# Conditioning chunks tied behind one weight split each, and the seven products of the values in another order

## The chip, the cores and the metric

The kernel runs on one core of a Trainium2 chip, in one launch. The metric is the device time in microseconds (us) of that launch; smaller is better. The engines meant below are TensorE (matmuls), the vector engine (VectorE), the scalar engine (ScalarE), GpSimd, and SyncE, which here does nothing but issue transfers. Each engine takes its instructions from a queue of its own, in order.

## The reference

Two layers of a block on 512 tokens of 1024 numbers each, float32 throughout. Layer 0 mixes tokens with a gated linear recurrence, layer 1 with dilated attention in three groups; each is followed by a gated feed-forward. Every norm is scaled, shifted and gated by a conditioning vector, which is a matrix of 1024 by 6144 times one vector:

```python
for layer in range(DEPTH):
    mod = (cond @ ada_w[layer] + ada_b[layer])[:, None, :]
    sh1, sc1, g1, sh2, sc2, g2 = jnp.split(mod, 6, axis=-1)
    u = rms_norm(h, norm_g[layer, 0]) * (1.0 + sc1) + sh1
    ...
    h = h + (1.0 + g1) * rms_norm(y, norm_g[layer, 1])
    u = rms_norm(h, norm_g[layer, 2]) * (1.0 + sc2) + sh2
    y = swiglu_ffn(u, ffn_w_in[layer], ffn_w_out[layer])
    h = h + (1.0 + g2) * rms_norm(y, norm_g[layer, 3])
```

The change lies in layer 1's attention:

```python
proj = (u @ w_in).astype(jnp.float32).reshape(B, S, N_GROUPS, 3, ATT_HEADS, ATT_HEAD_DIM)
for gi, (window, dilation) in enumerate(DILATED_GROUPS):
    q = apply_partial_rope(proj[:, :, gi, 0], cos, sin) * scale
    k = apply_partial_rope(proj[:, :, gi, 1], cos, sin)
    v = proj[:, :, gi, 2]
    o_g, lse_g = dilated_group_attention(q, k, v, window, dilation)
    ...
wts = jax.nn.softmax(jnp.stack(lses, axis=0), axis=0)
o = jnp.einsum('gbsh,gbshd->bshd', wts, jnp.stack(outs, axis=0))
```

with eight heads of 128 and the groups (128, 1), (512, 4) and (2048, 16).

## The kernel before

**Numbers.** A float32 product is made of three TensorE products of parts. A scalar-engine copy rounds a weight to a high part (`hi`, L123), a vector-engine subtraction gives the low part (`lo`, L124), and `three` (L446) issues hi by hi, hi by lo and lo by hi. So the last parts that a block of matmuls waits for are the low parts of its weights.

**Weights.** `Stream` holds one list of items for the whole program, in the order in which they are wanted. A "w" item is a weight tile of 1 MB: loaded by SyncE's queue into one of two raw tiles, then split into one of three pairs of parts. A "unit" is a block of the values' weights of 1024 by 512, in two tiles. An "ada" item is a chunk of a conditioning matrix (256 rows by 512 columns in this stage), a "rows" item a bias and norm row for a gate, a "do" item work without a load. `process_to` (L112) works through the list: where it meets a weight, it splits it; where it meets another item, it calls the item's function. `weave` puts the conditioning items among the weights: after weight number `first + n * every`, group n. For the weights of q and k the pair (first, every) is `ADA_AT` (L35).

**Conditioning beside q and k.** 24 chunks, two vector-engine products each (L282 for the first of a sum, else L284, 128x512), make six half vectors: scale, shift and gate of the second half of layer 1. When a half vector's eight products are done, GpSimd adds it over the partitions (L286), and a later item writes it into columns (L301) or, for the gate, into a row (L336, L337). During this stage the chunks have two tiles of their own ("side" tiles, from the pool opened as `a_side`), so they don't take raw tiles from the weights; `fill` loads into them as soon as one of the two is free, and `place` remembers which items were loaded so.

**Values, 680 to 781 us.** The product of 512 tokens by 1024 with 1024 by 512 weights is done per unit in the manner of Strassen, with seven products p1 to p7 of quarter size (24 matmuls of 256 columns each) instead of eight. Each needs a weight quarter or a sum of quarters: p1 takes q1, p2 and p3 take q3 (p3 after S4), p4 q2, p5 the sum S1 (L1605, here on the vector engine only for the second unit, on GpSimd for the later ones), p6 S2 (L1611, which needs S3, L1608), and p7 the q0 that S3 overwrote; S4 is L1614. `parts` splits such a quarter (scalar copy, then the low part `loq` on the vector engine, L1628). The products land in banks that are put together by `keep2`, `keep3` (scalar copies), `add4` (L1661) and `add5` (L1665) on the vector engine, `add1` (L1669) on GpSimd, and `out11`, `out12`, `out21`, `out22` (L1672 to L1681) on the vector engine. This stage is written out by hand: the four compute engines run it in the order of the calls.

**Heads, 781 to about 1150 us.** For each of 24 (head, group) pairs, one weight tile gives q and k (two blocks of 24 matmuls of 512 columns, L447 to L449), the scalar engine moves them out of the banks (L1827, L1828), the vector engine turns the first 32 rows (L1835 to L1838, "turning"), and two scalar copies (L1841) put these back into q and k. `Fillers` calls, a fixed number of blocks later, the scores (L1870 for the plain group, L1889 for the two others), their maxima (L1875, L1891) and exponentials, the merging of the groups (weights from L1910 on, products at L1926 and L1933), the transposes (L1938) and the products with V (L1963 to L1975). The order of calls is only a start here: the framework's scheduler works out with a model of its own in which order each engine gets these instructions, so the recorded order may differ from that of the code.

Of the kernel before, what the change touches and what calls it, by code (L numbers as in the profile page):

```python
# [9 lines left out]
F32 = mybir.dt.float32  # L10
# [23 lines left out]
R0 = 0  # L34
ADA_AT = (1, 0.85)  # L35


class Stream:
# [75 lines left out]
    def process_to(self, end):  # L114
        while self.done < end:
            self.fill()
            i = self.done
            kind = self.items[i][0]
            t = self.raw.pop(i)
            if kind == "w":  # L120
                hi = self.pool.tile([P, 2048], F32R, name=f"hi{i}", tag="hi", bufs=self.parts)
                lo = self.pool.tile([P, 2048], F32R, name=f"lo{i}", tag="lo", bufs=self.parts)
                self.nc.scalar.copy(hi, t)  # L123
                self.nc.vector.tensor_sub(lo, t, hi.bitcast(F32))  # L124
                self.ready.append((hi, lo))
            else:
                self.items[i][2](t)
# [63 lines left out]
def block_kernel(tc, x, c, positions, ada_w, ada_b, norm_g, hgrn_w_in, lower, hgrn_norm_g, hgrn_w_out,  # L191
# [6 lines left out]
    with ExitStack() as ctx:  # L198
# [223 lines left out]
        st = Stream(nc, wp, items, 2, 3)  # L422
        st.side_end = side_end

# [1127 lines left out]
        def values(turn):  # L1552
# [166 lines left out]
            b = Unit(UNITS[1])  # L1719
            b.S1(dve)  # L1720
            a.keep3()
            a.run("p6")
            b.S3()
            b.parts("p1")
            a.add4()
            a.add1()
            a.run("p7")
            b.S2()
            b.parts("p5")
            b.parts("p6")  # L1730
            a.add5()
            a.out12()
            a.run("p4")
            for n in range(1, len(UNITS)):
                last = a
                a, b = b, None
                a.hold()
                a.run("p1")
                a.parts("p2")
                last.out21()  # L1740
                a.run("p6")
                a.S4()
                a.keep2()
                last.out22()
                a.parts("p7")
                a.run("p5")
                a.parts("p3")
                a.add4()
                a.run("p2")
                a.keep3()  # L1750
                a.add1()
                a.parts("p4")
# [6 lines left out]
                a.run("p7")  # L1759
                a.out11()  # L1760
                if b:
                    b.parts("p1")
                    b.S3()
                a.run("p3")
                a.add5()
                if b:
                    b.S2()
                    b.parts("p6")
                a.run("p4")
                a.out12()  # L1770
                if b:
                    b.parts("p5")
            a.out21()
# [263 lines left out]
```

## Time and profile before

| what | value |
|---|---|
| time, median of 3 runs | 1526.21 us (1524.43 to 1528.13) |
| profiled execution, its own time | 1522.11 us |
| its span | 1520.4 us |
| mean granted TensorE clock | 0.997 |
| values stage | 680 to 781 us |
| heads stage | 781 to about 1150 us |

A row of the page's fifth part gives a group of instructions by line, engine and tile, its count, busy time and mean, and the idle time ahead of it with what ended that; these are the two lines that split a whole weight, over the whole program:

```profile
L124 DVE TENSOR_TENSOR lo<-raw,hi 128x2048 fp32r<-128x2048 f32 x65 | 152.1, 2340 | 103.6 <-ACT hi L123 96.1
L123 ACT CAST hi<-raw 128x2048 fp32r<-128x2048 f32 x65 | 124.0, 1908 | 150.9 <-DMA raw<-in_ffn_w_out_dram 51.3
```

And from the page's part on transfers (kind, engine, count, size, median time from issue to landing), the chunks of conditioning beside the weights of the same stage:

```profile
raw<-in_attn_w_in_dram SPq DMA_DIRECT2D x48, 512.0 KB, 5.2
...
side<-in_ada_w_dram SPq DMA_DIRECT2D x24, 512.0 KB, 5.1
```

In the prediction PE is TensorE, PEld its weight load, DVE the vector engine, ACT the scalar engine, POOL GpSimd and SP SyncE. "out<-in" names the tiles, without their numbers.

### The profile page before, as it was taken

The numbers are of one execution on the slowest core, as the hardware profiler recorded it, in microseconds if no ns is written. First come the engines' busy times: TensorE is split into PE (matmuls) and PEld (weight loads), VectorE is DVE, ScalarE is ACT, GpSimd is POOL, SyncE is SP. The second block draws the span as 40 slices with busy tenths as digits, with TensorE's granted clock in tenths as the row PEclk, the third lists the DMA queues.
The fourth block names the chain that finished last, engine by engine and source line by source line (L and its number), as shares of the span: only waits on it lengthen the run. The fifth ranks groups of instructions, "written<-read, shape, count | busy, mean of one in ns | idle before, by whom it ended". The sixth has DMA issues, their size and how long they took to land. (4 is left out here: it accounts for less than half of the span.)

```text
span 1520.4 us, 24054 instructions
## 1 busy us (share of the span) xinstructions
PE 1490.6 (98%) x9471; PEld 1315.2 (87%) x9471; DVE 1107.8 (73%) x1846; ACT 705.0 (46%) x1125; POOL 278.9 (18%) x237
## 2 busy tenths in 40 slices
PE   8999999999999999999999989999999999999998
PEld 6777888899999988889997778888888999999886
DVE  4587867588888886589967886655656978888633
ACT  4433443364444433364444556556555634554231
POOL 1011210051222211031213321001002222221100
PEclk9999999999999999999999999999999999999999
DMA  9654444324333456334478754334302233334531
GB/s 307 180 167 141 153 137 166 111 70 125 112 112 112 127 189 230 127 106 144 139 217 257 214 144 87 109 84 98 98 29 84 85 106 107 107 106 159 188 116 56
DMA packets 211202, 205.48 MB, mean 135 GB/s; under 512 B 7256, under 2 KB 167184, under 8 KB 211088
## 3 DMA queue, kind: packets, MB, share of 16 engines
q1 hardware_dynamic: 206192, 190.87, 40.7%
q0 software_dynamic: 4384, 12.72, 3.2%
q8 instruction: 74, 1.21, 0.3%
q10 hardware_dynamic: 512, 0.35, 0.1%
q14 instruction: 40, 0.33, 0.1%
HBM read 195.46 MB, written 8.45 MB: 134 GB/s over the span
## 5 line engine op out<-in xcount | busy, mean ns | idle before, releaser
L447 PE MATMUL ps_mm<-uh,hi 128*128 128x512 f32 (+1 forms) x784 | 290.6, 371 | 0.0
L449 PE MATMUL ps_mm<-uh,lo 128*128 128x512 f32 (+1 forms) x784 | 290.0, 370 | 0.0
L448 PE MATMUL ps_mm<-ul,hi 128*128 128x512 f32 (+1 forms) x784 | 289.5, 369 | 0.0
L124 DVE TENSOR_TENSOR lo<-raw,hi 128x2048 fp32r<-128x2048 f32 x65 | 152.1, 2340 | 103.6 <-ACT hi L123 96.1
L123 ACT CAST hi<-raw 128x2048 fp32r<-128x2048 f32 x65 | 124.0, 1908 | 150.9 <-DMA raw<-in_ffn_w_out_dram 51.3
L447 PEld LDWEIGHTS ps_mm<-uh,hi 128*128 128x128 f32 x784 | 148.0, 189 | 32.1 <-issue 8.4
L449 PEld LDWEIGHTS ps_mm<-uh,lo 128*128 128x128 f32 x784 | 148.4, 189 | 23.5
L448 PEld LDWEIGHTS ps_mm<-ul,hi 128*128 128x128 f32 x784 | 148.2, 189 | 22.9
L822 ACT CAST hiq<-raw 128x1024 fp32r<-128x1024 f32 x72 | 72.3, 1051 | 72.7 <-DVE raw L810 71.2
L447 PE MATMUL ps_mm<-hi,oh 128*128 128x512 f32 x240 | 94.2, 392 | 0.0
L448 PE MATMUL ps_mm<-lo,oh 128*128 128x512 f32 x240 | 93.6, 390 | 0.0
L826 DVE TENSOR_TENSOR loq<-raw,hiq 128x1024 fp32r<-128x1024 f32 x72 | 84.8, 1218 | 0.0
L806 POOL TENSOR_TENSOR raw<-raw 128x512 f32<-128x512 f32 x36 | 57.9, 1608 | 106.2 <-DVE loq L802 45.7
L810 DVE TENSOR_TENSOR raw<-raw 128x1024 f32<-128x1024 f32 x36 | 44.1, 1225 | 40.9 <-POOL raw L806 40.9
L286 POOL PARTITION_ALL_REDUCE shared<-shared x12 | 45.9, 3822 | 140.4 <-DVE shared L284 120.1
L449 PE MATMUL ps_mm<-hi,ol 128*128 128x512 f32 x176 | 68.5, 389 | 0.0
L856 POOL TENSOR_TENSOR shared<-shared 128x256 f32<-128x256 f32 x36 | 30.2, 839 | 205.6 <-DVE shared L855 205.6
L1841 ACT COPY qk<-turning 32x512 f32<-32x512 f32 x48 | 45.2, 942 | 47.6 <-DVE turning L1838 46.4
L447 PE MATMUL ps_mm<-sums,hiq 128*128 128x256 f32 x216 | 59.7, 277 | 0.1
L448 PE MATMUL ps_mm<-sums,hiq 128*128 128x256 f32 x216 | 59.7, 276 | 0.0
L449 PE MATMUL ps_mm<-sums,loq 128*128 128x256 f32 x216 | 59.7, 276 | 0.0
L447 PE MATMUL ps_a<-hi,oh 128*128 128x512 f32 x152 | 59.6, 392 | 0.0
(466 smaller groups left out, 4250.7 us busy)
## 6 DMA issues: line engine op xcount, KB each, us to landing
raw<-in_ffn_w_in_dram SPq DMA_DIRECT2D x144, 256.0 KB, 4.2
raw<-in_ada_w_dram SPq DMA_DIRECT2D x28, 1024.0 KB, 5.2
raw<-in_attn_w_in_dram SPq DMA_DIRECT2D x48, 512.0 KB, 5.2
raw<-in_ffn_w_out_dram SPq DMA_DIRECT2D x22, 1024.0 KB, 5.0
raw<-in_hgrn_w_in_dram SPq DMA_DIRECT2D x12, 1024.0 KB, 5.5
side<-in_ada_w_dram SPq DMA_DIRECT2D x24, 512.0 KB, 5.1
raw<-in_ffn_w_in_dram SPq DMA_DIRECT2D x8, 1024.0 KB, 5.1
first<-in_ada_w_dram SPq DMA_DIRECT2D x14, 512.0 KB, 7.7
```

Of the source, the lines that this page charges most:

```text
L123: self.nc.scalar.copy(hi, t)
L124: self.nc.vector.tensor_sub(lo, t, hi.bitcast(F32))
L286: pool.partition_all_reduce(a, a, P, bass.bass_isa.ReduceOp.add)
L447: pe.matmul(ps, ah, bh, start=start, stop=False)
L448: pe.matmul(ps, ah, bl, start=False, stop=False)
L449: pe.matmul(ps, al, bh, start=False, stop=stop)
L806: pool.tensor_add(r[:, 2], r[:, 2], r[:, 0])
L810: dve.tensor_tensor(r[:, 0:2], r[:, 0:3:2], r[:, 1:2].broadcast_to((P, 2, 512)), op=OP.add)
L822: act.copy(hi, src)
L826: dve.tensor_sub(lo, src, hi.bitcast(F32))
L856: pool.tensor_add(W[:, 3], W[:, 3], W[:, 5])
L1841: act.copy(*((dst, src) if g == 0 else (V4(dst), L4(src))))
```

## The change

It has two parts. In `Stream`, the vector instruction that makes the low part of a weight is remembered, and an item that was loaded into a side tile (a chunk or a gate's row) is worked on under `tc.issue_after` of that instruction: its instructions may stand only behind it in the scheduler's order. "do" items are not tied. `ADA_AT` goes from (1, 0.85) to (1, 0.87), so the 26 groups of items for 24 weights meet two at a weight at other places: 8, 15 and 22, where it was 7, 13 and 18 (counted from 0).

In `values`, the products after p1 run as p2, p5, p6, p7, p3, p4, where it was p6, p5, p2, p7, p3, p4; the parts are made in that order too, the sums S1, S3 and S2 of the second unit come later, in the later units S3 and S2 too, and the copies, additions and outputs stand where their banks are ready in the new order. In the first unit (`a` ahead of the loop), the order of the products stays. No instruction that computes is added or taken away. Lines behind L124 are three further down in the changed kernel.

```diff
--- before.py
+++ after.py
@@ -32,7 +32,7 @@
 C3 = float(np.float32(TWO_PI - C1 - C2))
 MAGIC = 12582912.0
 R0 = 0
-ADA_AT = (1, 0.85)
+ADA_AT = (1, 0.87)
 
 
 class Stream:
@@ -121,8 +121,11 @@
                 hi = self.pool.tile([P, 2048], F32R, name=f"hi{i}", tag="hi", bufs=self.parts)
                 lo = self.pool.tile([P, 2048], F32R, name=f"lo{i}", tag="lo", bufs=self.parts)
                 self.nc.scalar.copy(hi, t)
-                self.nc.vector.tensor_sub(lo, t, hi.bitcast(F32))
+                self.low = self.nc.vector.tensor_sub(lo, t, hi.bitcast(F32))
                 self.ready.append((hi, lo))
+            elif self.place.get(i):
+                with self.tc.issue_after(self.low.ins):
+                    self.items[i][2](t)
             else:
                 self.items[i][2](t)
             self.done += 1
@@ -420,7 +423,7 @@
         f1a, f1b = ffn_ws(1)
         items += f1a + weave(f1b[:9], ada_seq((1, 5)), 0) + f1b[9:]
         st = Stream(nc, wp, items, 2, 3)
-        st.side_end = side_end
+        st.side_end, st.tc = side_end, tc
 
         fl = Fillers()
 
@@ -1717,38 +1720,37 @@
             a.out11()
             st.load_unit(va)
             b = Unit(UNITS[1])
-            b.S1(dve)
             a.keep3()
             a.run("p6")
-            b.S3()
             b.parts("p1")
             a.add4()
             a.add1()
+            b.parts("p2")
             a.run("p7")
-            b.S2()
-            b.parts("p5")
-            b.parts("p6")
+            b.S1(dve)
             a.add5()
             a.out12()
+            b.parts("p5")
             a.run("p4")
+            b.S3()
+            b.S2()
             for n in range(1, len(UNITS)):
                 last = a
                 a, b = b, None
                 a.hold()
                 a.run("p1")
-                a.parts("p2")
                 last.out21()
-                a.run("p6")
+                a.parts("p6")
+                last.out22()
+                a.run("p2")
+                a.keep2()
                 a.S4()
-                a.keep2()
-                last.out22()
                 a.parts("p7")
                 a.run("p5")
+                a.out11()
                 a.parts("p3")
-                a.add4()
-                a.run("p2")
+                a.run("p6")
                 a.keep3()
-                a.add1()
                 a.parts("p4")
                 st.load_unit(va)
                 if n + 1 < len(UNITS):
@@ -1757,18 +1759,19 @@
                 else:
                     st.fill()
                 a.run("p7")
-                a.out11()
+                a.add4()
+                a.add1()
                 if b:
                     b.parts("p1")
-                    b.S3()
                 a.run("p3")
                 a.add5()
                 if b:
-                    b.S2()
-                    b.parts("p6")
+                    b.S3()
+                    b.parts("p2")
                 a.run("p4")
                 a.out12()
                 if b:
+                    b.S2()
                     b.parts("p5")
             a.out21()
             a.out22()
```

What this does to the queues, at three places. First, the vector engine's queue in the values, at the step from the first unit to the second, where the second unit's parts are made (`raw`, `other` and `s` are tiles of its weights, `hiq` and `loq` their parts, `w` the partial results, `ps_` banks, `vals` the result). Before:

```order
L1672 TENSOR_TENSOR vals_6424<-w_6454,ps_mm_6489 128x2x256
L1605 TENSOR_TENSOR s_6550<-raw_6228,other_6229 128x1024
L1608 TENSOR_TENSOR raw_6228<-raw_6228 128x4x256
L1628 TENSOR_TENSOR loq_6581<-raw_6228,hiq_6580 128x1024
L1661 TENSOR_TENSOR w_6584<-w_6454,ps_mm_6554 128x512
L1611 TENSOR_TENSOR raw_6228<-s_6550,raw_6228 128x4x256
L1628 TENSOR_TENSOR loq_6581<-s_6550,hiq_6580 128x1024
L1628 TENSOR_TENSOR loq_6617<-raw_6228,hiq_6616 128x1024
L1665 TENSOR_TENSOR w_6620<-w_6584,ps_mm_6588 128x512
L1675 TENSOR_TENSOR vals_6424<-w_6586,ps_a_6458 128x2x256
L1628 TENSOR_TENSOR loq_6617<-other_6229,hiq_6616 128x1024
```

And in the changed kernel:

```order
L1675 TENSOR_TENSOR vals_6424<-w_6454,ps_mm_6489 128x2x256
L1631 TENSOR_TENSOR loq_6579<-raw_6228,hiq_6578 128x1024
L1664 TENSOR_TENSOR w_6582<-w_6454,ps_mm_6553 128x512
L1631 TENSOR_TENSOR loq_6579<-other_6229,hiq_6578 128x1024
L1608 TENSOR_TENSOR s_6550<-raw_6228,other_6229 128x1024
L1668 TENSOR_TENSOR w_6614<-w_6582,ps_mm_6588 128x512
L1678 TENSOR_TENSOR vals_6424<-w_6584,ps_a_6458 128x2x256
L1631 TENSOR_TENSOR loq_6618<-s_6550,hiq_6617 128x1024
L1611 TENSOR_TENSOR raw_6228<-raw_6228 128x4x256
L1614 TENSOR_TENSOR raw_6228<-s_6550,raw_6228 128x4x256
L1681 SCALAR_TENSOR_TENSOR vals_6424<-w_6614,ps_mm_6621 128x2x256
L1631 TENSOR_TENSOR loq_6618<-raw_6228,hiq_6617 128x1024
```

The low parts of `raw` and `other` for the first two products now come first, one and three rows behind the output; the sums (L1605, L1608, L1611 before; L1608, L1611, L1614 now) moved behind them, and the low parts that need sums stand seventh and eleventh behind that output, where they stood sixth and seventh.

Second, the same engine in the heads, from the negated maxima of the first head's plain group on (`nN`; `sN`, `mR` are maxima, `side` the chunks' tiles, `shared` their sums, `lo` a low part of a weight, `rot` and `turning` the turning of q and k). Before:

```order
L282 TENSOR_SCALAR shared<-side_7773,cond 128x512
L337 SCALAR_TENSOR_TENSOR gate_8096<-gate_8096,side_7583 128x512
L1877 TENSOR_SCALAR nN_7717<-sN_7716 128x4
L1838 TENSOR_TENSOR turning_7712<-turning_7712,rot_7764 64x512
L284 SCALAR_TENSOR_TENSOR shared<-side_7773,cond,shared 128x512
L284 SCALAR_TENSOR_TENSOR shared<-side_7862,cond,shared 128x512 x2
L284 SCALAR_TENSOR_TENSOR shared<-side_7959,cond,shared 128x512 x2
L124 TENSOR_TENSOR lo_7865<-raw_7683,hi_7864 128x2048
L284 SCALAR_TENSOR_TENSOR shared<-side_8104,cond,shared 128x512
L1835 STREAM_SHUFFLE rot_7852<-turning_7808 64x512
```

And in the changed kernel:

```order
L1880 TENSOR_SCALAR nN_7717<-sN_7716 128x4
L1841 TENSOR_TENSOR turning_7712<-turning_7712,rot_7764 64x512
L124 TENSOR_TENSOR lo_7865<-raw_7683,hi_7864 128x2048
L285 TENSOR_SCALAR shared<-side_7773,cond 128x512
L1838 STREAM_SHUFFLE rot_7852<-turning_7808 64x512
L287 SCALAR_TENSOR_TENSOR shared<-side_7773,cond,shared 128x512
L1894 ISA PR_7811,mR_7812<-ps_a_7815,maskR 128x128
```

The five products of three chunks (`side_7773`, `side_7862`, `side_7959`) that stood ahead of the weight split L124 are gone from there: behind the split stand the two products of one chunk, and the gate's row (L337) isn't there any more.

Third, SyncE's queue, which issues the loads of the same stage (`raw` a weight, two transfers each; `side` a chunk or the gate's rows). Before:

```order
L73 DMA raw_7683<-in_attn_w_in_dram 128x8x128 x2
L75 DMA side_7773<-in_ada_w_dram 128x2x512
L75 DMA side_7862<-in_ada_w_dram 128x2x512
L73 DMA raw_7779<-in_attn_w_in_dram 128x8x128 x2
L69 DMA side_8099<-in_ada_b_dram 128x512
L69 DMA side_8099<-in_norm_g_dram 128x512
L75 DMA side_7959<-in_ada_w_dram 128x2x512
L75 DMA side_8104<-in_ada_w_dram 128x2x512
L75 DMA side_8224<-in_ada_w_dram 128x2x512
L73 DMA raw_7868<-in_attn_w_in_dram 128x8x128 x2
L75 DMA side_8232<-in_ada_w_dram 128x2x512
```

And in the changed kernel:

```order
L73 DMA raw_7683<-in_attn_w_in_dram 128x8x128 x2
L75 DMA side_7773<-in_ada_w_dram 128x2x512
L73 DMA raw_7779<-in_attn_w_in_dram 128x8x128 x2
L75 DMA side_7862<-in_ada_w_dram 128x2x512
L73 DMA raw_7868<-in_attn_w_in_dram 128x8x128 x2
L75 DMA side_7959<-in_ada_w_dram 128x2x512
L73 DMA raw_7965<-in_attn_w_in_dram 128x8x128 x2
L69 DMA side_8102<-in_ada_b_dram 128x512
L69 DMA side_8102<-in_norm_g_dram 128x512
L75 DMA side_8107<-in_ada_w_dram 128x2x512
L73 DMA raw_8226<-in_attn_w_in_dram 128x8x128 x2
```

Weights and chunks now take turns; before, two or three chunks followed each other.

## The prediction

> **What bounds the kernel now.** I read the page's first part, then the waits of TensorE over both places of the change, then what the vector engine waits for there, then windows by stage.
>
> ```profile
> PE 1490.6 (98%) x9471; PEld 1315.2 (87%) x9471; DVE 1107.8 (73%) x1846; ACT 705.0 (46%) x1125; POOL 278.9 (18%) x237
> ```
>
> TensorE is busy for 98% of a span of 1520.4 us. The change adds and removes no instruction that computes, so it can only act on the 29.8 us in which TensorE waits, and on time lost at a lower clock. Waits of TensorE, 640 to 1180 us (total, times, longest):
>
> ```profile
> PE ps_a L1889 <- ACT qk L1841: 4.4, 2, 2.3
> PE ps_mm L448 <- DVE loq L1628: 2.9, 2, 1.8
> PE ps_a L1938 <- DVE PN L1933: 2.8, 1, 2.8
> PE ps_b L1973 <- ACT pt L1942: 1.6, 1, 1.6
> PE ps_a L1938 <- DVE PR L1926: 0.9, 1, 0.9
> PE ps_a L1870 <- DVE mR L1891: 0.7, 1, 0.7
> PE ps_a L1938 <- issue: 0.4, 1, 0.4
> PE ps_a L1870 <- ACT qk L1841: 0.4, 1, 0.4
> PE ps_a L1938 <- ACT pt L1942: 0.4, 1, 0.4
> ```
>
> The second row is the values (two waits, so 1.1 and 1.8). The others lie in the heads; all but the 1.6 us fall between 819 and 916 us. What holds the vector engine from 780 to 925 us (two rows of its waits), and when the conditioning products run:
>
> ```profile
> DVE shared L284 <- DMA side<-in_ada_w_dram: 13.5, 6, 5.0
> ```
>
> ```profile
> DVE gate L336 <- POOL shared L286: 2.5, 1, 2.5
> ```
>
> ```profile
> L284 DVE SCALAR_TENSOR_TENSOR shared<-side,cond,shared x42: 731/746/753, 787.3 to 898.2; 128x512 f32<-128x512 f32 x42
> ```
>
> All 48 products of the 24 chunks (these 42 and 6 that open a sum) are over by 899 us, in the first third of a stage that runs from 780 to about 1150 us. The vector queue is in order, so each wait for a chunk's transfer, 13.5 us in all, and the wait for GpSimd's sum, 2.5, hold up the turning, the maxima and the weight splits behind them. Stage by stage (time, TensorE, its weight loads, vector, scalar, GpSimd busy; clock; DMA):
>
> ```profile
> 740.00:760.00 20.00, 20.00 (x175) 20.00 (x174) 17.94 (x17) 8.30 (x10) 5.40 (x3) 1.00 0.39 107
> 825.00:845.00 20.00, 17.93 (x80) 14.62 (x79) 17.11 (x32) 7.07 (x9) 4.53 (x3) 0.96 0.66 194
> 960.00:1000.00 40.00, 40.00 (x208) 34.14 (x207) 23.82 (x72) 23.48 (x43) 3.36 (x5) 1.00 0.35 90
> ```
>
> Later units of the values (first row) and heads without chunks (last row) have TensorE full; the heads with chunks don't. TensorE is the bound, and the vector queue sets its holes.
>
> **The change, part 1: the chunks in the heads.** Here are the two largest holes ahead of scores; first the vector engine, in order of time (start, length, instruction, wait ahead of it):
>
> ```profile
> 816.13 0.68 DVE L1838 TENSOR_TENSOR turning<-turning,rot 64x512 f32<-64x512 f32 x1
> 816.74 2.31 DVE L284 SCALAR_TENSOR_TENSOR shared<-side,cond,shared 128x512 f32<-128x512 f32 x3
> 824.00 1.54 DVE L284 SCALAR_TENSOR_TENSOR shared<-side,cond,shared 128x512 f32<-128x512 f32 x2 [4.95 <-DMA side<-in_ada_w_dram]
> 825.46 2.28 DVE L124 TENSOR_TENSOR lo<-raw,hi 128x2048 fp32r<-128x2048 f32 x1
> ```
>
> Then the scalar engine's weight copy and turned copies, and TensorE:
>
> ```profile
> 821.67 1.90 ACT L123 CAST hi<-raw 128x2048 fp32r<-128x2048 f32 x1
> ...
> 835.64 2.21 ACT L1841 COPY qk<-turning 32x512 f32<-32x512 f32 x2 [9.82 <-DVE turning L1838]
> ```
>
> ```profile
> 818.75 0.39 PE L449 MATMUL ps_mm<-uh,lo 128*128 128x512 f32 x1
> 818.98 0.39 PE L447 MATMUL ps_mm<-uh,hi 128*128 128x512 f32 x1
> 821.70 1.16 PE L1889 MATMUL ps_a<-qk,qk 128*128 128x128 f32 x8 [2.34 <-ACT qk L1841]
> ...
> 837.91 1.16 PE L1889 MATMUL ps_a<-qk,qk 128*128 128x128 f32 x8 [2.07 <-ACT qk L1841]
> ```
>
> The scores at 837.91 waited for copies, these for a turning that ended at 835.6, and this stood behind products whose transfer landed 4.95 us late. In the new queue one chunk follows each weight split, and the chunks of the next three weights are no longer ahead of it. Walked with the same durations: the first turning loses the 2.5 us wait for GpSimd's sum ahead of it, so the copies that let TensorE go at 821.70 end at 819.2; TensorE, whose scores stand one matmul earlier (0.23 us, the distance of the first two rows), comes at 821.70 - 2.34 - 0.23 = 819.1. The next weight copy then ends at 819.2 + 1.9 = 821.1 and its split, free of the 4.95 us, at 823.4. Behind the split stand now one chunk's two products, a shuffle, four maxima and three steps of 0.6 us (816.74 - 816.13); at 0.74 for the second product, some 0.4 for the first (it opens a sum), 0.6 for the shuffle and 0.8 for the maxima (estimates by the steps' length) that is 4.3 us: 827.7, the copies 829.9. TensorE arrives 42 matmuls and 0.9 us of scores after 819.1: 829.7. So both holes (4.4 us) shrink to 0.1 to 0.2 each.
>
> The other holes (the merges' 2.8 and 0.9, the maxima's 0.7, three of 0.4) stand at 850 to 916 us behind the same queue with its chunk waits. Holes that go: 4.4 + 2.8 + 0.9 + 0.7 + 0.4 + 0.4 + 0.4 = **10.0 us**. The clock comes on top (two windows by the view's columns as above; clock is the third number from the end):
>
> ```profile
> 823.10:826.40 3.30, 3.30 (x9) 2.52 (x9) 2.37 (x3) 2.62 (x5) 0.00 (x0) 0.50 0.80 154
> 881.20:884.40 3.20, 3.20 (x11) 2.76 (x11) 3.11 (x4) 0.58 (x1) 1.35 (x1) 0.50 0.71 177
> ```
>
> Shortly after the holes of 2.3 and 2.8 us the granted clock is 0.50 for the length of such a window; after that of 2.07 us it isn't. If the holes cause it, 3.30 x 0.5 + 3.20 x 0.5 = **3.2 us** go with them. [...] The rows show half clock behind the two longest holes of the stage and nowhere else in it, so I go by the rows.
>
> What is late next: every unit now carries two products between its weight split and the sum of its turning, up to 2 x 0.74 = 1.5 us. The heads without chunks had 23.8 of 40 us of vector work, so the sum is no problem; the chain is. Its slack before, in such a head (one row of the scalar engine, one of TensorE):
>
> ```profile
> 1039.67 2.21 ACT L1841 COPY qk<-turning 32x512 f32<-32x512 f32 x2 [1.83 <-DVE turning L1838]
> ```
>
> ```profile
> 1041.59 0.61 PE L1889 MATMUL ps_a<-qk,qk 128*128 128x128 f32 x4
> ```
>
> None: the copies end as the scores start. But the recorded order also moves TensorE: counted in matmuls of the blocks ahead of them, the scores of the dilated groups stand 5 to 17 later than before from the fourth head to the seventh (1.1 to 3.9 us), and 1 to 36 earlier in the first three. So later heads get cover for the 1.5 us, and in the early ones the queue must run as walked. No row shows this mix, so I bound the new holes by rows: 0 (heads without chunks) and 13.2 (as much as now, clock included); I take **1.5**, near the first, since the walk came out at 0.1 to 0.2. Transfers: on the sync queue each chunk now stands behind one weight and is asked for a unit ahead of use, no longer three in a row. The chunks' last sums end ahead of the last unit's split, so nothing waits for them at the output product.
>
> **Part 2: the values.** Only the step from the first unit to the second had holes (TensorE, vector, GpSimd).
>
> ```profile
> 698.80 0.28 PE L447 MATMUL ps_mm<-hiq,uh 128*128 128x256 f32 x1
> 700.20 0.39 PE L448 MATMUL ps_mm<-loq,uh 128*128 128x256 f32 x1 [1.11 <-DVE loq L1628]
> ```
>
> ```profile
> 696.53 1.22 DVE L1605 TENSOR_TENSOR s<-raw,other 128x1024 f32<-128x1024 f32 x1
> 697.78 1.23 DVE L1608 TENSOR_TENSOR raw<-raw 128x1024 f32<-128x1024 f32 x1
> 698.93 1.22 DVE L1628 TENSOR_TENSOR loq<-raw,hiq 128x1024 fp32r<-128x1024 f32 x1
> ...
> 701.79 2.32 DVE L1628 TENSOR_TENSOR loq<-s,hiq 128x1024 fp32r<-128x1024 f32 x1
> ```
>
> ```profile
> 700.90 2.13 POOL L1669 TENSOR_TENSOR w<-w,w 128x512 f32<-128x512 f32 x1 [19.59 <-DVE w L1661]
> ```
>
> The first low part stood behind two sums (1.2 each), the second product's behind seven operations. Now the first two products need no sum and their low parts come first: 696.53 + 1.2 = 697.7, ahead of TensorE's 698.9, so the 1.11 goes. The work isn't less, though, only due later: ahead of the low part of p6, now fourth, stand three low parts, four steps of 0.6 us and three sums. With its own that is 4 x 1.15 + 4 x 0.6 + 3 x 1.2 = 10.6 us from 696.53, and 1.1 more for the one that GpSimd's addition stretches from 1.2 to 2.3: 707.1 to 708.2. TensorE gets there after three products: in the row of 740 us a matmul takes 20 / 175 = 0.114 us, a product of 24 so 2.74, three 8.2, and 698.8 + 8.2 + 0.1 = 707.1: a hole of 0 to 1.1. The low part of p7, behind one more sum, can cost as much again, and more if GpSimd stretches that too. So 2.9 us become 0 to 3.4; I take 2.2 (twice 1.1), a gain of **0.7**, between -0.5 and 2.9. Later units: TensorE was full with vector work of 17.9 of 20 us, and GpSimd's sum, now ahead of its addition, stretches one or two low parts by 1.1 each, which the 2.1 us left cover: 0.
>
> **Sum.** 10.0 + 3.2 - 1.5 + 0.7 = 12.4 us off the profiled execution's 1522.1 (span 1520.4), 1509.7; that execution was 4.1 us below the median of the shown runs, 1526.2, and from the median it is 1513.8. Best case, all holes, the clock, the values and the 1.6 at the stage's end: 13.2 + 2.9 + 1.6 = 17.7, 1508.5.
>
> **Rivals.**
> - *Half of it stays.* The holes behind 850 us (5.6 us, with one half-clock window 1.6) hang on the merges' chain of small steps and an exponential, not on a chunk's transfer, and return. Then 1526.2 - (12.4 - 7.2) = 1521.0. For it: none of these rows names a transfer. Against: the heads from 960 us have the same merges and no hole. 15%.
> - *The clock rule.* The half-clock windows have another cause and stay: 1513.8 + 3.2 = 1517.0. 5%; the rows stand against it.
> - *Slower: chunks on a chain without slack.* If TensorE's later places don't cover, each of the 15 units from the fourth head on pays the 1.5 us ahead of its copies: 22 us for 13.2 won, 1526.2 + 9 = 1535. It decides at 13.2 / 15 = 0.9 us a unit. The later places (1.1 us at least) stand against it. 6%.
> - *No change.* The early heads, where TensorE's scores stand up to 36 matmuls (8 us) sooner, grow holes as large as the old ones: 1524 to 1527. For it: the walk leaves no slack there. 8%.
>
> **How the numbers follow.** The forecast has 66%, its own range 1508.5 to 1517. To leave out no more than two in ten the range goes up to the half case: 1508 to 1521.5. Faster or slower by 0.2%, 3.05 us, is about what a measurement of this kernel can tell from no change: forecast, clock and half case give 86% faster; same 8%; slower 6%.
>
> **What would show it.** Right: products of the chunks spread from 787 to over 1100 us; no vector wait for the side transfer over 1 us; no hole over 1 us of TensorE from 785 to 1110 us and clock 1.00 in every window of it; in the values one or two holes, now at p6 or p7, of at most 3.4 us. Wrong: holes in front of the scores in most units (the chain), holes at the merges after 850 us (the half case), or half-clock windows without a long hole ahead of them (the clock rule).

## The result, and the profile after

The changed kernel takes **1512.55 us** (median of 4 runs, 1509.69 to 1515.20) where the kernel before takes 1525.32 (4 runs, 1522.43 to 1528.13): a ratio of 0.9916, with a 95% interval of 0.9889 to 0.9943. The prediction was 1513.8, in a range of 1508.0 to 1521.5. The profiled execution took 1512.30 us, with a span of 1510.6.

First the page's line of busy times of the changed kernel, then its waits of TensorE from 640 to 1180 us (total, times, longest):

```profile
PE 1488.0 (99%) x9471; PEld 1315.4 (87%) x9471; DVE 1115.3 (74%) x1846; ACT 706.1 (47%) x1125; POOL 274.5 (18%) x237
```

```profile
PE ps_a L1892 <- ACT qk L1844: 3.3, 3, 1.5
PE ps_mm L451 <- DVE loq L1631: 3.0, 2, 2.1
PE ps_b L534 <- DVE xn L528: 1.6, 1, 1.6
PE ps_b L1976 <- ACT pt L1945: 0.4, 1, 0.4
PE ps_mm L450 <- ACT hiq L1629: 0.2, 1, 0.2
```

In the heads and at their end 3.7 us of holes are left of 11.6 (the first and the fourth row; the third lies behind, at 1169 us, and the kernel before has it too, past the stretch shown). In the values nothing is won: 3.2 us in place of 2.9. Then the vector engine's waits from 780 to 925 us, and the products of the chunks:

```profile
DVE lo L124 <- ACT hi L123: 34.0, 10, 7.2
DVE wZ L1918 <- ACT wE L1916: 7.1, 4, 3.1
DVE vals L1678 <- PE ps_mm L452: 0.7, 1, 0.7
DVE PR L1894 <- PE ps_a L1892: 0.5, 1, 0.5
```

```profile
L287 DVE SCALAR_TENSOR_TENSOR shared<-side,cond,shared x42: 722/740/759, 790.7 to 1058.2; 128x512 f32<-128x512 f32 x42
```

No wait for a chunk or for GpSimd is left; the vector engine now waits where it does no harm, for the next weight's high part. The products end at 1059 us instead of 899. The same stretch of 110 us, first of the kernel before, then of the changed one (columns as in the prediction's windows):

```profile
790.00:900.00 110.00, 101.32 (x467) 83.08 (x466) 84.61 (x200) 53.54 (x83) 31.94 (x18) 0.97 0.78 228
```

```profile
790.00:900.00 110.00, 107.76 (x519) 90.01 (x518) 75.94 (x188) 58.52 (x103) 17.37 (x16) 1.00 0.69 194
```

Before, the vector engine was busy for 84.6 us, and with 15.2 us of waits for chunks, 2.5 for GpSimd and 7.5 for TensorE (its waits in this stretch) it had no free time at all. TensorE's loss, 8.7 us of idle time and what the lower clock cost, is here.

Where the 9.8 us between the two spans come from, in us, by the first matmul of each stage in the timeline. All stage lengths below are of this kind; "rest" runs from the first matmul of the output product to the end, and the last heads' small matmuls still run in it:

| kernel | up to the values | values | heads | rest |
|---|---|---|---|---|
| before | 679.1 | 101.6 | 333.9 | 405.8 |
| changed | 682.1 | 102.0 | 322.6 | 403.9 |

Heads and rest gain 13.2 us (333.9 + 405.8 less 322.6 + 403.9), the values lose 0.4. The 3.0 us lost ahead of the values are not the change's: up to there the order of all five queues is the same. In this one execution the granted clock was 0.50 from 16.9 to 23.8 us, two stretches of 3.4 us, and in the profiled execution of before it was 1.00 there. Over all fourteen profiles of this case, the four with two such stretches reach the values at 680.3 to 682.1 us, the ten with one or none at 677.9 to 679.6; so these stretches go with most of the 3.0 us, and the rest is spread between executions.

### The profile page after: what moved, and what is told of

Read it like the earlier page. It is cut to its first block, busy times and chain, and to the rows that moved or that the text cites. A ratio compares the mean times of both kernels' runs of the same rounds, so it can differ in the third digit from the quotient of the medians.

```text
span 1510.6 us, 24044 instructions
## 1 busy us (share of the span) xinstructions
PE 1488.0 (99%) x9471; PEld 1315.4 (87%) x9471; DVE 1115.3 (74%) x1846; ACT 706.1 (47%) x1125; POOL 274.5 (18%) x237
## 4 chain that ended last, share of the span: by engine, by line
PE 79%; DVE 9%; ACT 5%; issue 2%; DMA 2%; POOL 1%; SPq 1%; DVEq 0%; POOLq 0%; ACTq 0%
PE ps_mm L450 16%; PE ps_mm L452 16%; PE ps_mm L451 16%; PE ps_b L450 3%; PE ps_b L451 3%; PE ps_b L452 3%; PE ps_a L450 3%; PE ps_a L452 3%; PE ps_a L451 3%; PE ps_mm L1202 2%; ACT junk L489 1%; ACT qk L1844 1%; DVE loq L1631 1%; PE ps_a L1202 1%; DVE lo L124 1%
## 5 line engine op out<-in xcount | busy, mean ns | idle before, releaser
L124 DVE TENSOR_TENSOR lo<-raw,hi 128x2048 fp32r<-128x2048 f32 x65 | 152.2, 2342 | 106.6 <-ACT hi L123 106.5
L289 POOL PARTITION_ALL_REDUCE shared<-shared x12 | 42.0, 3498 | 127.3 <-DVE shared L287 127.3
```

The source lines that it names most:

```text
L124: self.low = self.nc.vector.tensor_sub(lo, t, hi.bitcast(F32))
L289: pool.partition_all_reduce(a, a, P, bass.bass_isa.ReduceOp.add)
```

## The experiments

A table of what ran; ratios are against runs of the kernel before on the same chip, with 95% intervals, and the stages are those of the one profiled execution.

| kernel | median us | ratio | values | heads | rest |
|---|---|---|---|---|---|
| tie alone | 1513.32 | 0.9919 [0.9900, 0.9939] | 101.4 | 327.5 | 405.8 |
| tie and places | 1509.67 | 0.9896 [0.9878, 0.9915] | 101.7 | 323.6 | 403.9 |
| values alone | 1525.67 | 1.0005 [0.9990, 1.0020] | 103.5 | 333.0 | 405.7 |
| holes made | 1519.47 (one run) | | 110.8 | 323.2 | 404.0 |
| another step in the values | 1508.13 | 0.9882 [0.9866, 0.9899] | 99.3 | 322.9 | 404.0 |
| sums behind the turning | 1509.76 | 0.9890 [0.9875, 0.9905] | 102.1 | 321.9 | 405.8 |
| both of these | 1505.05 | 0.9859 [0.9844, 0.9873] | 99.3 | 318.5 | 405.8 |
| products twice | 1510.82 (one run) | | 102.0 | 322.2 | 403.6 |
| chunks in twos | 1510.04 | 0.9900 [0.9877, 0.9923] | 103.5 | 323.3 | 404.0 |
| chunks in threes | 1514.38 | 0.9932 [0.9914, 0.9951] | 103.5 | 323.2 | 406.9 |
| changed kernel again | 1512.41 | 0.9920 [0.9903, 0.9937] | 103.5 | 324.7 | 403.9 |
| chunks crowded, tied | 1520.01 | 0.9984 [0.9967, 1.0001] | 103.5 | 333.1 | 405.8 |

### The parts of the change

The tie alone, on the kernel before:

```diff
-                self.nc.vector.tensor_sub(lo, t, hi.bitcast(F32))
+                self.low = self.nc.vector.tensor_sub(lo, t, hi.bitcast(F32))
                 self.ready.append((hi, lo))
+            elif self.place.get(i):
+                with self.tc.issue_after(self.low.ins):
+                    self.items[i][2](t)
...
-        st.side_end = side_end
+        st.side_end, st.tc = side_end, tc
```

> The tie alone, on the kernel before: old places (1, 0.85), old order of the values. Theory Q (the vector queue: chunks that waited for their transfer held up splits and turnings): the heads go from 333.9 us to about 323, as in the changed kernel (322.6), since one chunk still stands behind each split but for two places where two meet; no vector wait for a side transfer over 1 us; values stay at 101.6; in all about 11 us less than before. Theory P (the places 0.87 did it, by moving which weights meet two groups): the heads stay above 330.

The heads took 327.5 us, between the two forecasts. There is one wait for a chunk, of 2.4 us, where theory Q had none over 1. With the same list as before, the chunks' products now run from 786 to 1049 us, where untied they ran from 787 to 899. The tie with the new places:

```diff
-ADA_AT = (1, 0.85)
+ADA_AT = (1, 0.87)
```

> Part 1 of the change whole (tie and places 0.87), with the old order of the values. Heads 322 to 324 us by both theories. Against the tie alone it prices the places: theory Q expects no more than 2 us between the two. If the values' new order is worth what the prediction said (0.7 us), this kernel's values stage is 0.7 longer than that of the changed kernel; by the two profiles so far (101.6 before, 102.0 after) it is 0.4 shorter.

Heads of 323.6 us: the places are worth 3.9 us in these two profiles, more than the 2 that Q allowed. Most of that is the clock: with the tie alone a hole of 2.3 us at 819.6 us, and two of 0.6 and 1.5 close behind each other at 912 us, are each followed by a window at half clock (1.7 us each); with the new places the clock is 1.00 in both stages. Whether a hole is followed by such a window varies between executions (see "What halves the clock"), so what the places are worth by themselves is not shown by these two profiles. The places without the tie were not run: built so, the program has the same order in all five queues as before.

The values' order alone (as an edit of the changed kernel):

```diff
-ADA_AT = (1, 0.87)
+ADA_AT = (1, 0.85)
...
-                self.low = self.nc.vector.tensor_sub(lo, t, hi.bitcast(F32))
+                self.nc.vector.tensor_sub(lo, t, hi.bitcast(F32))
                 self.ready.append((hi, lo))
-            elif self.place.get(i):
-                with self.tc.issue_after(self.low.ins):
-                    self.items[i][2](t)
...
-        st.side_end, st.tc = side_end, tc
+        st.side_end = side_end
```

> The values' new order alone. Theory S (the wait is moved, not removed): values 102.0 us against 101.6 before, two holes of about 0.9 and 2.1 us at p6 and p7 of the second unit in place of 1.1 and 1.8; heads as before, 333 to 335 us; no difference in all that can be measured. Rival: the new order helps the heads by what it leaves to them (the vector engine ends the values earlier), then heads under 332.

No difference in all, as theory S has it, and heads as before. But the values took 103.5 us, not 102.0: behind the hole of 2.1 us at p7 a window ran at half clock. Nine profiles have the new order at this step (the one with holes made in later units is among them). Five of them show that window, and 103.5 us; the other four have the same two holes without it. Of three with the old order none has it (101.4 to 101.7). So part 2 costs 0.4 us, and 1.5 more in about every second execution. Part 1 alone takes 1509.67 us (1509.60 to 1510.54), the changed kernel 1512.55 and 1512.41. The times point the same way, though the intervals of the ratios overlap.

### What makes the holes in the heads

Every product of a chunk done twice:

```diff
                         dve.scalar_tensor_tensor(a, r[:, k], sc, a, op0=OP.mult, op1=OP.add)
+                    if l == 1 and v in (2, 3, 4):
+                        dve.scalar_tensor_tensor(a, r[:, k], sc, a, op0=OP.mult, op1=OP.add)
```

> The changed kernel with every product of the chunks beside q and k done twice on the vector engine, which changes the conditioning of the last feed-forward: some 1.4 us more on the chain of each unit with a chunk (24 units). Theory slack (TensorE's places leave the chain room): heads 323 to 328 us. Theory no slack (the rival of the prediction: what comes onto the chain is paid unit by unit): heads 322.6 + 24 x 1.4 less what 0.9 us a unit would cover, 24 x 0.5 = 12, so 335 or more.

The theory of slack holds: 322.2 us in its one profile, below the 323 to 328 that it gave and no more than with single products. The window of 110 us:

```profile
790.00:900.00 110.00, 108.18 (x523) 90.47 (x523) 89.46 (x207) 59.62 (x104) 17.56 (x17) 1.00 0.68 188
```

The vector engine is busy for 89.5 us, more than the 84.6 of before, and TensorE has 108.2. So it is not vector work that made the holes. Left are the waits inside the queue. Chunks woven in twos and threes at the same mean rate (k stands for 2 and for 3):

```diff
-        items += weave([aqk(g, hd) for hd in range(NH) for g in range(3)], ada_seq((1, 2), (1, 4), (1, 3), n=2), *ADA_AT)
+        groups = ada_seq((1, 2), (1, 4), (1, 3), n=2)
+        groups = [sum(groups[j:j + k], []) for j in range(0, len(groups), k)]
+        items += weave([aqk(g, hd) for hd in range(NH) for g in range(3)], groups, ADA_AT[0], ADA_AT[1] * k)
```

> The changed kernel with its chunks woven in twos: two behind every second weight split instead of one behind nearly each. Two side tiles, so both chunks can have landed before they are asked for. Theory T (what made the holes was the third chunk in a row, whose tile comes free only with the first one's last product, so that the queue waits a whole transfer of 5 to 6 us): no vector wait for a side transfer over 1.5 us, heads 322 to 325 us (322.6 in the changed kernel). Theory M (mere number: four products of 0.74 us behind one split are too much for the turning): holes at the scores of every second unit, heads over 328.

> The same in threes: three chunks behind every third split. Theory T: in each of the eight groups the third chunk is waited for, 3 to 6 us each, most of it ahead of a turning or a split: 20 to 40 us of vector waits for side transfers, holes of TensorE back, half clock behind some of them, heads 328 to 336 us (333.9 before). Theory M or any by which spreading matters only in the mean: heads as in twos.

> The changed kernel once more, beside these two, as their base: heads 322 to 323.5 us, values 101.9 to 102.1 without a half-clock window behind p7 and 103.5 with one; 1509 to 1514 us.

Twos: the heads take 323.3 us, as T has it, though with one wait of 2.6 us where T had none over 1.5; M, with over 328, falls. Threes: T fails. The vector engine does wait for third chunks (780 to 1120 us, chunks in threes):

```profile
DVE shared L287 <- DMA side<-in_ada_w_dram: 7.7, 4, 4.4
DVE shared L285 <- DMA side<-in_ada_w_dram: 4.1, 2, 3.8
```

but these are 11.8 us, not 20 to 40, over 330 us, and the heads take 323.2. A wait of 4 us by itself did not cost here: the two longest, 3.8 and 4.4 us, stand at 997 and 1039 us, and behind them only one hole, of 0.3 us, comes before the output product. The place may count too: a wait of 2.2 us in the first head, at 806 us, was followed by a hole of 1.3. The changed kernel again gave 324.7 against 322.6 the first time, from the same program: in this execution the fifth product of a chunk, in the middle of a turning, waited 1.8 us for its transfer from 803 us on, and holes of 0.9 and 2.3 us follow it. Six of the twelve profiles with tied chunks have a hole of 0.8 to 1.7 us ahead of the first plain scores; in each of them that fifth product waited 1.5 to 2.6 us, and in the six others it did not.

So the chunks were crowded again, with the tie in place:

```diff
-ADA_AT = (1, 0.87)
+ADA_AT = (1, 0.4)
```

> The changed kernel with the tie kept but the chunks woven closely again, at (1, 0.4): 26 groups behind the first eleven weights. Theory R (the rate: 24 chunks in about nine weights' time, with two tiles, are asked for faster than their transfers land, so that the vector queue waits 15 us or more for them and for GpSimd within 110 us, and these waits come out as holes): vector waits for side transfers over 10 us in all, heads 329 to 335 us, half clock behind the holes over 2 us that fall into one clock window. Theory O (what counts is that the tie keeps a chunk behind a split, never ahead of it): heads 323 to 326 us, as with chunks in twos and threes (323.3 and 323.2).

Theory R holds: heads of 333.1 us, nearly the 333.9 of before. The waits of the vector engine, 780 to 925 us, and of TensorE, 640 to 1180 us (the rows of the heads):

```profile
DVE shared L287 <- DMA side<-in_ada_w_dram: 10.7, 4, 4.7
DVE shared L285 <- DMA side<-in_ada_w_dram: 2.6, 3, 1.6
DVE gate L339 <- POOL shared L289: 2.5, 1, 2.5
```

```profile
PE ps_a L1892 <- ACT qk L1844: 8.6, 3, 3.4
...
PE ps_a L1941 <- DVE PN L1936: 1.3, 2, 1.0
PE ps_a L1873 <- ACT qk L1844: 0.8, 1, 0.8
```

The 24 chunks are back within about 126 us, and waits and holes as large as those of before with them, though most holes now stand at the scores and only 1.3 us of them at the merges. So the tie gains next to nothing by what stands behind what; it gains by keeping the scheduler from drawing the chunks forward, so that the rate written in the list is the rate in the queue. A close rate also brings all chunks into the early heads; rate and place are not told apart by these runs.

### The holes that are left

Two groups of rows of the changed kernel, the vector engine and GpSimd, first in the values and then in the heads (start, length):

```profile
712.37 1.22 DVE L1617 TENSOR_TENSOR other<-other,raw 128x1024 f32<-128x1024 f32 x1
713.50 3.55 DVE L1631 TENSOR_TENSOR loq<-raw,hiq 128x1024 fp32r<-128x1024 f32 x1
```

```profile
713.56 2.40 POOL L1608 TENSOR_TENSOR s<-raw,other 128x1024 f32<-128x1024 f32 x1
```

```profile
814.56 0.68 DVE L1839 TENSOR_TENSOR rot<-rot,shared 64x512 f32<-64x512 f32 x1
815.16 2.72 DVE L1840 TENSOR_TENSOR turning<-turning,shared 64x512 f32<-64x512 f32 x1
```

```profile
814.77 3.58 POOL L289 PARTITION_ALL_REDUCE shared<-shared  x1 [15.05 <-DVE shared L287]
```

p7's low part takes 3.55 us instead of 1.2 beside GpSimd's sum for the third unit, and ends about 1.1 us after it (713.56 + 2.40 = 715.96, and 713.50 + 3.55 = 717.05). A step of a turning takes 2.72 us instead of 0.68 beside GpSimd's sum over the partitions; all six of these sums do this to one step (2.72 or 2.73 us each). In the first pair of rows the low part ends about one full length (1.2) behind GpSimd's sum, though it is the low part that is recorded as starting first, by 0.06 us. In the second pair the step ends at 815.16 + 2.72 = 817.88 us, ahead of the end of GpSimd's sum at 814.77 + 3.58 = 818.35, so it was not held up for the whole of that instruction as recorded. What holds the vector engine up beside GpSimd is not shown by these rows.

An edit of the values' step that moves operations out of GpSimd's way:

```diff
             b.parts("p1")
+            b.S1(dve)
             a.add4()
             a.add1()
             b.parts("p2")
             a.run("p7")
-            b.S1(dve)
             a.add5()
-            a.out12()
             b.parts("p5")
             a.run("p4")
             b.S3()
             b.S2()
+            a.out12()
...
                 a.parts("p6")
-                last.out22()
+                if n > 1:
+                    last.out22()
                 a.run("p2")
                 a.keep2()
-                a.S4()
+                if n > 1:
+                    a.S4()
                 a.parts("p7")
+                if n == 1:
+                    last.out22()
+                    a.S4()
```

> The changed kernel with another order of the vector engine at the step from the first to the second unit of the values only: S1 ahead of the low part of p2 (so that GpSimd's addition does not run against S1), the two outputs behind S2, and p7's low part ahead of S4 and of the last output (so that it ends before GpSimd's sum for the third unit starts). Theory G (the two holes left, 0.9 and 2.1 us, are the low part of p6 late behind a sum that GpSimd held up, and that of p7 held up by GpSimd's sum, 3.55 us in place of 1.22): holes of together under 1 us, values 99.5 to 100.5 us (102.0 in the changed kernel). Theory W (the vector engine has simply too much to do there): holes of 2 to 3 us, only at other products, values 101.5 to 102.5.

Theory G holds: 99.3 us, one hole of 0.7. The low part of p7 now takes 1.23 us again, three microseconds ahead of GpSimd's sum (vector engine, then GpSimd, in that profile):

```profile
709.34 1.23 DVE L1631 TENSOR_TENSOR loq<-raw,hiq 128x1024 fp32r<-128x1024 f32 x1 [0.21 <-ACT hiq L1629]
```

```profile
712.28 2.42 POOL L1608 TENSOR_TENSOR s<-raw,other 128x1024 f32<-128x1024 f32 x1
```

Next, the six sums over the partitions behind the turning:

```diff
+        sums_due = []
...
-                if kt == KT - 1 and (l, v) != (0, 5):
+                if kt == KT - 1 and l == 1 and v in (2, 3, 4):
+                    sums_due.append(a)
+                elif kt == KT - 1 and (l, v) != (0, 5):
                     pool.partition_all_reduce(a, a, P, bass.bass_isa.ReduceOp.add)
...
-            dve.tensor_add(both, both, rot)
+            turned = dve.tensor_add(both, both, rot)
+            while sums_due:
+                a = sums_due.pop()
+                with tc.issue_after(turned.ins):
+                    dve.tensor_scalar(a[:, 0:1], a[:, 0:1], 1.0, None, op0=OP.mult)
+                pool.partition_all_reduce(a, a, P, bass.bass_isa.ReduceOp.add)
```

> The changed kernel with GpSimd's six sums of the chunks over the partitions made to wait for the end of the turning of their unit (a vector step of one column on the sum, behind the turning's last step). Theory G (three of the four holes left in the heads, 1.3, 0.5, 1.5 us, come from such a sum that holds up one vector step of the turning by 2.05 us): no step of a turning over 1 us any more, no hole over 0.5 us at the scores, heads 319 to 320.5 us (322.6 in the changed kernel). Theory C (the holes are the chain's own, one chunk's 1.5 us): holes as before, heads 322 to 323.5; the steps that wait for the sum, on the vector engine behind it, could also bring new holes.

By its mechanism G holds: no step of a turning is over 1 us, and the holes at the scores of the dilated groups are 0.2 and 0.5 (1.3, 0.5 and 1.5 before this edit). By its sum it doesn't: the heads take 321.9 us, not 319 to 320.5. A late transfer (1.7 us) made a hole of 1.5 at the first plain scores, and a hole of 1.7 at the stage's end, which the kernel before had too, is back and falls under "rest". Both edits together:

> Both of these edits on the changed kernel, as a version that may beat it. If both theories G hold, the holes from the values to the output product come to under 1.5 us, and the time is 1506 to 1508 us; if neither, 1510 to 1513.

1505.05 us (1504.86 to 1506.00), below the 1506 to 1508 forecast for it, and the fastest here. Its waits of TensorE, 640 to 1180 us, whole:

```profile
PE ps_b L1989 <- ACT pt L1958: 1.7, 1, 1.7
PE ps_b L537 <- DVE xn L531: 1.6, 1, 1.6
PE ps_mm L454 <- DVE loq L1634: 0.7, 1, 0.7
PE ps_a L1905 <- ACT qk L1857: 0.4, 1, 0.4
```

Why the hole at the stage's end comes and goes with the scheduler's order was not tried.

### What halves the clock

Holes made in the values, by extra vector steps that change no value:

```diff
+            LONGER = {2: 4, 3: 3, 4: 2}
...
+                for _ in range(LONGER.get(n, 0)):
+                    dve.tensor_tensor(a.q1, a.q1, a.q1, op=OP.max)
                 a.parts("p6")
```

> The changed kernel with idle time made for TensorE in the values, where its order is fixed: before the parts of p6, 4, 3 and 2 extra vector steps of 1.1 us (a maximum of a tile with itself, which changes no value) in the third, fourth and fifth unit. The low part of p6 was 0.7 to 3 us early there, so holes of about 2.5, 2 and 1 us are expected, and perhaps a few small ones behind them. Theory H (a long hole is followed by a window at half clock, as behind those of 2.3 and 2.8 us before): half clock behind the hole of over 2.3 us, none behind that of 1 us. Theory N (the half-clock windows of before had another cause): clock 1.00 everywhere in the values, whatever the holes.

The sizes came out otherwise: 0.9 and 2.1 us in the second unit (as in the changed kernel), 0.9 and 2.1 in the third, 0.2 and 2.2 in the fifth. N falls: the clock is 0.50 behind the hole of 2.2. But H as put falls too: behind the two holes of 2.1 it stays 1.00. The half-clock stretches of one execution start at multiples of 3.413 us from each other (in the profile of the kernel before 823.06 and 881.09, 17 apart; of the values alone 714.68 and 823.91, 32 apart; of the chunks crowded, tied 842.01 and 923.93, 24 apart), so time was cut into windows of that length for each execution, and TensorE's busy time read in them. Chunks crowded, tied (second number of busy time: TensorE; clock third from the end):

```profile
821.53:824.94 3.41, 2.02 (x9) 1.32 (x8) 2.31 (x4) 3.40 (x10) 0.12 (x1) 1.00 0.57 172
824.94:828.35 3.41, 1.80 (x12) 1.67 (x13) 0.00 (x0) 3.36 (x4) 1.59 (x2) 1.00 0.97 319
828.35:831.76 3.41, 3.41 (x17) 2.81 (x16) 3.15 (x3) 2.23 (x5) 0.17 (x1) 1.00 0.52 134
838.60:842.01 3.41, 0.47 (x3) 0.05 (x1) 2.19 (x4) 1.77 (x2) 0.00 (x0) 1.00 1.14 313
842.01:845.42 3.41, 2.93 (x11) 2.74 (x12) 1.82 (x3) 3.37 (x4) 0.00 (x0) 0.50 0.44 161
920.52:923.93 3.41, 1.27 (x9) 0.81 (x8) 3.16 (x19) 2.80 (x3) 0.26 (x1) 1.00 0.00 0
923.93:927.34 3.41, 3.41 (x13) 2.83 (x12) 1.57 (x13) 1.02 (x5) 0.00 (x0) 0.50 0.02 5
```

A hole of 3.0 us that falls on two windows (1.4 and 1.6 idle) is followed by full clock; one of 2.1 that lies in one window is followed by half. Over the values and heads of all profiles whose windows can be placed, each of the 13 windows with 1.99 us idle or more (3.41 - 1.42 in the least of them, with chunks in twos, from 710.92 us) is followed by one at 0.50. Of those with 1.4 to 1.8 us idle only one is (1.71 us, where the rest was the attention's small matmuls), and none between 1.8 and 1.99 was seen. The hole of 2.07 us of the kernel before, behind which the clock stayed at 1.00, fits this too: counted from the half-clock window at 823.1 us, a border lies at 836.7, inside that hole (835.84 to 837.91), and leaves 0.9 and 1.2 us of it to the two windows.

## Why the prediction was right, and where it was not

**Holes that go, 10.0 us.** Right in place and cause. The holes of 2.8, 0.9, 0.7 and 0.4 at the merges and maxima all went, and the rival "half of it stays" fell. That each hung on the chunks is shown for their sum: crowding the chunks again cost as much in the heads, but brought back only 1.3 us at the merges. The walk, too, named the wait for GpSimd's sum and that for the transfer as what has to go; both went. But its reason, "one chunk follows each weight split", is only half of it: twos and threes do as well, and the same chunks crowded behind splits do not. The rate counts. The hole of 1.6 us at the stage's end, which the sum left standing and only the best case counted, went as well; the runs show it come and go, and not why.

**New holes, 1.5 us.** The mechanism was mis-sized: 3.7 us (1.3, 0.5, 1.5 and 0.4). What the walk left out was that GpSimd's sums now run beside steps of the turning and stretch one by 2.05 us each; with these sums moved, the holes at the scores were 0.2 and 0.5. Two of the new holes, 1.3 and 1.5, are over the 1 us that the prediction allowed.

**The clock, 3.2 us.** Gone in the heads, as forecast (3.4 by two whole windows of 3.41 us): no window of the heads is at half clock in either profile of the changed kernel. With that the rival "the clock rule", in which the half-clock windows have another cause and stay, fell; no row of this case had spoken for another cause. The reading by the holes' length alone (half clock behind 2.3 and 2.8 us, none behind 2.07) was too simple. By windows, the kernel before was idle for 2.05 of 3.41 us from 819.65 us on and for 2.78 from 877.68 on, ahead of its two windows at half clock, and the hole of 2.07 fell on two windows. The 13 windows that were idle for 1.99 of their 3.41 us or more were all followed by half clock.

**Slower: a chain without slack.** It fell: doubled products cost nothing (heads of 322.2 us, and 322.6 in the changed kernel). By the estimate of 1.4 us for the doubled products, TensorE's later places, or the free time between units, cover at least 1.4 us a unit more.

**No change in the early heads.** The walk left 0.1 to 0.2 us a hole, and 1.3 and 0.5 came, in the second execution 0.9, 2.3 and 0.5 with a late transfer, where 4.4 stood before: the place was right, the size was not.

**The values, a gain of 0.7 us.** Wrong in sign: a loss of 0.4 us, and 1.9 with the half-clock window. The step that failed is "the low part of p7 ... can cost as much again, and more if GpSimd stretches that too": the sum took 1.1 us for it, and it cost 2.1, because GpSimd's sum for the third unit comes just there; with the low part moved ahead of that sum the hole was gone. p6's hole, 0.9, was within its 0 to 1.1. That a half-clock window could follow the hole of 2.1 us, as it did in five of nine profiles, was not thought of. The window's 1.5 us lies outside the bounds given for this term.

**The sum.** Against the profiled execution, heads and rest gained 13.2 us where 11.7 were forecast, the values lost 0.4 where a gain of 0.7 was, and 3.0 us were lost at the program's start, which nobody could forecast from one profile. Of the 13.2, holes are 7.9 (1.6 of them the hole at the stage's end) and the clock 3.4. The other 1.9 is not idle time but busy time of TensorE, nearly all of it in the heads: there it fell by 5.1 us, from 324.0 to 318.9, with the same matmuls, and the clock explains 3.4 of that. The remainder was not followed up. That the total came out within 1.3 us of the median, then, is partly luck: new holes of 3.7 where 1.5 were forecast and a loss in the values were about made up by the 1.6 and the 1.9, which the sum did not have. The sign that the chunks' products would spread to over 1100 us was off as well (1059 us), without harm.

## What to carry to other kernels

In this kernel, work beside a tight chain was paid not by its busy time but by what its engine's queue waited for: 89.5 us of vector work in 110 us, with the products done twice, went with heads of 322.2 us, and 84.6 us of it with 15.2 us of waits for chunks went with heads of 333.9. So spread such work at a rate that its transfers can keep, and see in the recorded order that the scheduler has kept that rate. When an operation is moved, look at what other engines run beside its new place: here a part of what was won came back, as GpSimd's sums beside vector steps (2.72 us instead of 0.68, and 3.55 instead of 1.2), and moving these was worth another 7 us (1505.05 us, against 1512.55 and 1512.41).

## What the hardware showed that was not expected

- In the values and heads of these profiles the granted clock was 0.50 for one window of 3.41 us after each of the 13 windows in which TensorE was idle for 1.99 us or more (1.99 with chunks in twos, 2.94 from 838.60 us on with chunks crowded and tied), and after one window with 1.71; behind a longer hole across the border of two windows (3.0 us, split into 1.4 and 1.6, chunks crowded and tied) it stayed at 1.00. So a hole of 2.1 us cost 2.1 or 3.6 us (values of 102.0 and 103.5 us), by chance, and the same program varies by this: at its start the profiled executions had none, one or two such windows, and those with two came to the values 0.7 to 4.2 us later than the others.
- GpSimd's sum over the partitions, 3.6 us long, held up one vector step by 2.05 us (six times in the changed kernel); a sum of two 128x1024 tiles on GpSimd, 2.4 us long, stretched a vector subtraction from 1.22 to 3.55.
